# One-core hybrid transformer block: the planner's view of small operations, a group's last squares summed in PSUM, the memory norm one head sooner, a keys unit in a score bank

## The chip, the cores and the metric

The kernel runs as one program on one core of a Trainium2 chip. The metric is the device time of an execution in microseconds; before the change the median of three runs is 766.26 us (766.15 to 769.48).

## The reference

One layer of a streaming encoder on `x` of 512 x 1024 and 256 memory tokens, all float32. Three sub-layers follow each other, each with an RMS norm before it, one after it, and a residual.

1. The token mixer. `h = rms_norm(x)`, one projection `h @ w_in`, whose columns give queries, keys and values for 8 heads of forgetting attention and 8 heads of chunked attention (64 columns a head), and a forget gate. In both kinds
```
s = einsum(q, k) * scale + bias;  s = where(valid, s, NEG_INF)
p = softmax(s);  o = einsum(p, v)
```
over key positions up to the query's own (chunk). The 512 columns of each kind of head are normed by themselves (`rms_norm(o_f, g_fox_out)`, `rms_norm(o_c, g_chunk_out)`), put side by side and multiplied by `w_out`.
2. Cross-attention of 4 heads into the memory: `m = rms_norm(mem, g_mem_kv)`, keys and values from `m @ w_kv`, queries from the normed stream, softmax, output projection `w_o`.
3. A SwiGLU feed-forward: `(silu(g) * u) @ w_down`.

## The kernel before

**Products in three parts.** Float32 products are made of fp32r halves. A number is split into `hi` (a cast) and `lo = number - hi`, and each product is three matmuls, hi·hi, lo·hi and hi·lo (`mm3`, L398 to L402). Weights come in units of 128 x 1024 that are loaded by SyncE's queue (`raw`), cast by ScalarE (`hi`, L381) and subtracted by VectorE (`lo`, L382).

**The attention part.** The 16 heads are worked off in four groups of four: two groups of forgetting heads (n = 0, 1), then two of chunked heads (n = 2, 3), so head 15 is the third head of the last group. `head` (L782 to L828) goes over four query blocks of 128 rows. For each it makes the scores on TensorE (L791, L792) into a PSUM bank of kind `s`; VectorE adds the bias and finds the row's extreme in one instruction (L795, tiles `p` and `nm`); ScalarE takes the exponential (L805); VectorE inverts the row sum (L806, `rc`) and scales (L807); TensorE transposes `p` into a bank of kind `t` (L810); ScalarE casts that to `pth` (L812) and VectorE subtracts for `ptl` (L813). After the four blocks TensorE multiplies `pth` and `ptl` with the values (L819, bank `o`), and ScalarE and VectorE put the result (`ot`, `o`) in place. There are 3 banks of kind `a`, 2 of `s`, 2 of `t` and 1 of `o`.

**After two heads** `pair_out` (L830 to L839) makes `oh` and `ol` for the output projection, and GpSimd (POOL) squares `o`. The first pair's squares go to `sq`; the second pair of a kind, and each later one, squares `o` in place and adds it to `sq` (L839). `group_rs` (L841 to L849) then sums the squares over the partitions with four small matmuls against a column of ones (L844), one for each 128 rows, and makes the reciprocal root of the mean.

**The memory norm.** At n = 3 the memory is loaded (`mm`), squared, and the squares summed (`msq`). `mem_norm` (L851 to L858), traced ahead of the third head of that group, sums over the partitions (L512), makes the reciprocal root, spreads it over the partitions by a matmul (L521), multiplies `mm` in place in eight VectorE instructions (L854), and splits the result in `mT`: hi by ScalarE (L857), lo by VectorE (L858). `mT` is what the keys of the cross-attention are made from: four units of 48 matmuls of 256 columns each (L941 to L962), each unit in a bank `a`, result in `kT`. Ahead of them in the text stands the first half of the output projection (`mix`, L905 to L916, operands `oh`, `ol`, 512 columns), behind them the second half. Four row blocks of `x` are loaded by GpSimd's queue (`xo`).

**What sets the order.** Nothing above is issued in the order of the text. Everything traced ahead of the feed-forward's loop goes through `planned_order` (L90 to L280), a list scheduler. It walks through the program with a model of each engine's time and gives each engine a fixed order: of the instructions that can start at an engine's next free time, the one with the lowest number in the trace order, shifted by `later(n)`, goes first. The model's costs are `duration` (L126), `SIGNAL` and `TO_PE` (L45), the time until TensorE sees another engine's result, and `halves` (L152): when the start partitions of an instruction on VectorE, ScalarE or GpSimd differ from those of the one before, it is charged 28 ns after the former one's end, else it may start a little ahead of that end. `halves` counts operands of more than 8 elements a partition only, so a 128 x 1 operation among wide ones counts as another place. The feed-forward behind the planned part is written out by hand, and is not touched.

Of the kernel before, what the change touches and what calls it, by code (L numbers as in the profile page):

```python
# [8 lines left out]
F32 = mybir.dt.float32  # L9
F32R = mybir.dt.float32r  # L10
AF = mybir.ActivationFunctionType
ALU = mybir.AluOpType
AX = mybir.AxisListType

P = 128
SEQ = 512
# [25 lines left out]
    (ENGINES.DVE, ENGINES.Pool): 80.0, (ENGINES.Activation, ENGINES.Pool): 67.0,  # L42
    (ENGINES.Pool, ENGINES.DVE): 36.0, (ENGINES.Pool, ENGINES.Activation): 34.0,
}
TO_PE, LANDED = 247.0, 60.0  # L45


def number(dims):
    n = 1
    for d in dims:  # L50
        n *= d[1]
    return n
# [37 lines left out]
def planned_order(tc, instructions, homes):  # L90
# [35 lines left out]
    def duration(i):  # L126
        kind = type(i).__name__
        n = number(list(i.outs[0].bass_ap.ap)[1:])
        read = [number(list(a.bass_ap.ap)[1:]) for a in i.ins if tile_of(a)]
        columns = sum(n > 8 and m == 1 for m in read)  # L130
        if i.engine == ENGINES.PE:
            return MATMUL * n if n > 128 else 108.0 if n == 128 else 26.0
        if i.engine == ENGINES.Activation:
            return (284.0 if len(i.outs) > 1 else 160.0) + 0.838 * n + 80.0 * columns
        if i.engine == ENGINES.Pool:
            if n <= 8:
                return 174.0 if kind == "InstTensorCopy" else 1450.0 if n == 1 else 1040.0
            return 25.0 + (0.96 if kind == "InstMemset" else 2.0) * n
        if kind == "InstCustomDveAnt":
            return 245.0 + 0.99 * n  # L140
        if kind == "InstTensorReduce":
            return 158.0 + 1.02 * read[0]
        if kind == "InstMemset":
            return 70.0 + 0.8 * n
        if kind == "InstReciprocal" or n < 8:
            return 158.0
        full = [a for a in i.ins if tile_of(a) and number(list(a.bass_ap.ap)[1:]) > 8]
        if len(full) < 2 and not any(map(in_psum, full)):
            return 213.0 + 0.526 * n
        return 150.0 + 1.046 * n + 60.0 * columns  # L150

    def halves(i):  # L152
        starts = []
        for a in [i.outs[0]] + list(i.ins):
            ap = getattr(a, "bass_ap", None)
            if ap is not None and ap.ap[0][0] and number(list(ap.ap)[1:]) > 8:
                starts.append(ap.offset // ap.ap[0][0])
        return tuple(starts[:2])

    nodes = [i for i in instructions if type(i).__name__ not in ("BassTilePoolBoundary", "InstRegisterMove")]  # L160
    written, read, touched, uses, guests, previous, last_of = {}, {}, {}, {}, {}, {}, {}
# [70 lines left out]
    while any(ready.values()):  # L232
        best = None
        for e, waiting in ready.items():
            starts = [(t, k) for t, k in ((may_start(k), k) for k in waiting) if t is not None]
            if not starts:
                continue
            now = max(free.get(e, 0.0), min(starts)[0])
            if best is None or (now, str(e)) < best[:2]:
                best = now, str(e), e, *min((k, t) for t, k in starts if t <= now + 1.0)  # L240
        _, _, e, k, t = best
        ready[e].remove(k)
        i, start = nodes[k], max(free.get(e, 0.0), t)
        transfer = type(i).__name__ == "InstDMACopy"
        if transfer:
            free[e] = start + ISSUE
            end = landed[e] = max(start + 1900.0, landed.get(e, 0.0)) + 4 * number(i.outs[0].bass_ap.ap) / 300.0
            if e == ENGINES.Pool:
                end += 1500.0
        elif e == ENGINES.PE:  # L250
            cost = duration(i)
            waited = t > free.get(e, 0.0) + 5.0 and cost > 100.0
            free[e] = start + cost + (95.0 if waited else 0.0)
            end = start + max(cost, 60.0) + 170.0
        else:
            if halves(i) != place.get(e, (0, 0)):
                start = max(start, ends.get(e, 0.0) + 28.0)
            place[e] = halves(i)
            end = ends[e] = start + duration(i)
            free[e] = max(start + 20.0, end - TAIL[e])  # L260
        order.setdefault(e, []).append(i)
        for name in used[k]:
            if name not in lasts:
                lasts[name] = {}
                room[homes.tiles[name]].pop(0)
            lasts[name][e, transfer] = end
            uses[name] -= 1
            if not uses[name]:
                room[homes.tiles[name]].append(name)
        for j, in_turn in after[k].items():  # L270
            other = nodes[j].engine
            at[j] = max(at[j], start if in_turn else (start if e == other == ENGINES.PE else end) + reached(e, other, transfer))
            missing[j] -= 1
            if not missing[j]:
                ready.setdefault(other, []).append(j)
# [15 lines left out]
def hybrid_block_kernel(  # L291
# [31 lines left out]
    def bank(tag):  # L323
        serial[0] += 1
        return ps.tile([P, 512], F32, tag=tag, name=f"ps_{tag}{serial[0]}", bufs=BANKS[tag])
# [161 lines left out]
    with tc.tile_pool(name="mix", bufs=1, reuse_waits="tile") as bp:  # L487
# [339 lines left out]
                act.copy(tmp[own, :], acc[other, :])  # L827
                dve.tensor_tensor(out=o[own, :], in0=acc[own, :], in1=tmp[own, :], op=ALU.add)  # L828

        def pair_out(o, gc, oh, ol, sq, first, total):  # L830
            act.activation(oh, o, AF.Copy, scale=gcol(gc))
            dve.scalar_tensor_tensor(
                out=ol, in0=o, scalar=gcol(gc), in1=f32(oh), op0=ALU.mult, op1=ALU.subtract
            )
            if first:
                pool.tensor_tensor(out=sq, in0=o, in1=o, op=ALU.mult)
            else:
                pool.tensor_tensor(out=o, in0=o, in1=o, op=ALU.mult)
                pool.tensor_tensor(out=total, in0=sq, in1=o, op=ALU.add)  # L839

        def group_rs(sq, name):  # L841
            ss = bank("t")
            for t in range(NT):
                pe.matmul(ss[:, t : t + 1], sq[:, t * P : (t + 1) * P], ones, start=True, stop=True)  # L844
            ms = small(NT, "gms")
            dve.tensor_scalar(
                out=ms, in0=ss[:, :NT], scalar1=1.0 / 512.0, scalar2=None, op0=ALU.mult
            )
            return rstd_of(ms, NT, name)  # L849
# [16 lines left out]
        for n, (side, g) in enumerate(order):  # L866
            with later(-20):
                q, kt, kl, v = group_proj(f"{side}{g}")
            if n == 3:
                mT = big.tile([P, 2, KB, NMEM], F32R, tag="sB", name="mT")  # L870
                mm = bp.tile([P, KB, NMEM], F32, tag="V", name="mm", bufs=2)
                nc.gpsimd.dma_start(mm, mem_t.rearrange("(k p) n -> p k n", p=P))
                msq = bp.tile([P, 4, NMEM], F32, tag="T", name="msq", bufs=3)
                for k in range(0, KB, 2):
                    b = msq[:, 2 * (k > 0) : 2 * (k > 0) + 2, :]
                    act.activation(b, mm[:, k : k + 2, :], AF.Square, scale=1.0 / 32.0)
                    if k:
                        pool.tensor_tensor(out=msq[:, 0:2, :], in0=msq[:, 0:2, :], in1=b, op=ALU.add)
            if n == 0:
                gate = forget_gate()  # L880
                oh = ox.tile([P, 8, SEQ], F32R, tag="x1", name="oh")
                ol = ox.tile([P, 8, SEQ], F32R, tag="x2", name="ol")
            if n % 2 == 0:
                sqs.append(bp.tile([P, SEQ], F32, tag="sq", name=f"sq{side}", bufs=1))
            if n == 2:
                with later(300):
                    rs_g.append(group_rs(sqs[0], "rsg0"))
            for b in range(2):
                pr = 2 * g + b
                o = bp.tile([P, SEQ], F32, tag="o", name=f"o{side}{pr}", bufs=2)  # L890
                for h in range(2):
                    hh = 2 * pr + h
                    if n == 3 and 2 * b + h == 2:
                        mem_norm()
                    with later(urge[n] - 295):
                        bias = fox_bias(hh, *gate) if side == 0 else chunk_bias(hh)
                    with later(urge[n]):
                        head(q[b], kt[b], kl[b], v, 2 * b + h, h, bias, o)
                with later(urge[n]):
                    pair_out(  # L900
                        o, (G_FOX, G_CHK)[side] + pr, oh[:, 4 * side + pr, :], ol[:, 4 * side + pr, :],
                        sqs[side], n % 2 == 0 and b == 0, sqs[side],
                    )

        mix = big.tile([P, NT, D], F32, tag="sA", name="mix")  # L905
        with later(-5):
# [12 lines left out]
    with tc.tile_pool(name="cross", bufs=1, reuse_waits="tile") as cp:  # L919
# [21 lines left out]
        with later(-115):  # L941
            for c in range(4):
                hi, lo = unit()
                acc = bank("a")
                for b in range(2):
                    for k in range(KB):
                        cs = slice(b * P, (b + 1) * P)
# [398 lines left out]
        def halves(a):  # L1346
            return a.rearrange("p (t n) -> p t n", t=2)
# [448 lines left out]
```

## Time and profile before

| | |
|---|---|
| median of three runs | 766.26 us |
| the profiled execution | 766.12 us |
| its span, first to last instruction | 764.0 us |
| mean granted TensorE clock | 0.990 |
| TensorE (PE) busy | 747.9 us, 98% |
| VectorE (DVE) busy | 604.2 us, 79% |
| ScalarE (ACT) busy | 444.2 us, 58% |
| GpSimd (POOL) busy | 63.8 us, 8% |
| read from memory | 77.13 MB |

The profile is one execution. A row of a timeline is: start in us, length, engine, line, operation, output<-inputs, size, number of instructions taken together, and in brackets the idle time ahead of it with the instruction that ended it. The number of columns of a matmul is the second of the two sizes. Matmuls are pipelined: one may start before the former has ended, so their pace is read from start to start and not from their lengths. `PEld` is the load of a matmul's stationary operand, beside the matmuls. A row of TensorE's waits is: line, the engine and line waited for, us in total, times, the longest.

### The profile page before, as it was taken

What the parts mean: (1) busy time and instruction counts of PE and PEld (TensorE: products, weight loads), DVE (VectorE), ACT (ScalarE), POOL (GpSimd) and SP (SyncE); (2) the same over time, 40 slices, a digit from 0 to 9 for tenths busy, and PEclk for the clock granted to TensorE, in tenths of its full rate; (3) what the DMA queues carried; (4) which work ended last, traced back from release to release, by engine and by line L of the source; (5) the groups of instructions that cost most, each with busy time, mean ns of one, the idle gap of its engine ahead of it and who ended that gap; (6) DMA issues with size and microseconds to landing.
All of it is one profiled execution on the core that took longest, in us unless ns stands there. A gap on an engine that the chain in (4) does not pass through costs nothing.

```text
span 764.0 us, 12979 instructions
## 1 busy us (share of the span) xinstructions
PE 747.9 (98%) x5024; PEld 682.6 (89%) x5024; DVE 604.2 (79%) x1103; ACT 444.2 (58%) x818; POOL 63.8 (8%) x105
## 2 busy tenths in 40 slices
PE   9999999999989999999999999999999999999996
PEld 9988988888868988888878999999999999999995
DVE  8668899789877578655655598999999999998756
ACT  7558889566955448444564445555555557644321
POOL 1001232100410301000001200000000000000001
PEclk9999999999997999999999999999999999999998
DMA  7522222421412745332341015333333322233222
GB/s 251 149 74 82 55 59 68 110 98 57 138 55 63 250 158 165 112 94 63 121 131 60 28 33 162 111 112 111 112 112 111 111 85 83 83 138 111 84 83 110
DMA packets 60748, 80.05 MB, mean 105 GB/s; under 512 B 2704, under 2 KB 43664, under 8 KB 60688
## 3 DMA queue, kind: packets, MB, share of 16 engines
q1 hardware_dynamic: 59264, 74.49, 31.0%
q0 software_dynamic: 1280, 4.72, 1.7%
q8 instruction: 39, 0.64, 0.4%
q14 instruction: 21, 0.17, 0.1%
q10 hardware_dynamic: 144, 0.02, 0.0%
HBM read 77.13 MB, written 2.10 MB: 104 GB/s over the span
## 4 chain that ended last, share of the span: by engine, by line
PE 88%; issue 4%; ACT 3%; DVE 3%; POOL 1%; DVEq 0%; POOLq 0%; ACTq 0%
PE ps_a L399 14%; PE ps_a L400 14%; PE ps_a L402 14%; PE ps_t L1388 3%; PE ps_t L1385 3%; PE ps_s L1388 3%; PE ps_t L1386 3%; PE ps_s L1386 3%; PE ps_s L1385 3%; PE ps_o L819 3%; PE ps_s L402 2%; PE ps_s L400 2%; PE ps_s L399 2%; PE ps_t L810 2%; PE ps_a L1386 1%
## 5 line engine op out<-in xcount | busy, mean ns | idle before, releaser
L382 DVE TENSOR_TENSOR lo<-raw,hi 128x1024 fp32r<-128x1024 f32 x56 | 69.3, 1242 | 19.3 <-ACT hi L381 19.1
L399 PE MATMUL ps_a<-hTh,hi 128*128 128x512 f32 x192 | 76.5, 399 | 0.2 <-DVE z L618 0.2
L402 PE MATMUL ps_a<-hTh,lo 128*128 128x512 f32 x192 | 76.5, 398 | 0.0
L400 PE MATMUL ps_a<-hTl,hi 128*128 128x512 f32 x192 | 76.3, 397 | 0.0
L381 ACT CAST hi<-raw 128x1024 fp32r<-128x1024 f32 x56 | 57.9, 1049 | 27.2 <-PE ps_a L400 17.5
L1181 DVE TENSOR_TENSOR ring_lo<-sums,ring_hi 128x1024 fp32r<-128x1024 f32 (+1 forms) x39 | 46.7, 1197 | 11.8 <-ACT ring_hi L1180 7.2
L1180 ACT CAST ring_hi<-sums 128x1024 fp32r<-128x1024 f32 (+1 forms) x39 | 40.2, 1030 | 16.5 <-PE ps_s L1386 16.5
L1180 ACT CAST ring_hi<-fraw 128x1024 fp32r<-128x1024 f32 (+1 forms) x26 | 26.5, 1031 | 32.7 <-DVE fraw L1267 24.0
L805 ACT ACTIVATE p<-p,nm 128x128 f32<-128x128 f32 (+1 forms) x64 | 36.3, 568 | 11.3 <-DVE nm L795 10.9
L399 PEld LDWEIGHTS ps_a<-hTh,hi 128*128 128x128 f32 x192 | 36.2, 188 | 6.5 <-ACT V L607 0.4
L402 PEld LDWEIGHTS ps_a<-hTh,lo 128*128 128x128 f32 x192 | 36.2, 188 | 6.3
L400 PEld LDWEIGHTS ps_a<-hTl,hi 128*128 128x128 f32 x192 | 36.2, 188 | 6.1
L1181 DVE TENSOR_TENSOR ring_lo<-fraw,ring_hi 128x1024 fp32r<-128x1024 f32 (+1 forms) x26 | 31.0, 1203 | 11.3 <-ACT ring_hi L1180 11.3
L813 DVE TENSOR_TENSOR ptl<-ps_t,pth 128x128 fp32r<-128x128 f32 (+1 forms) x64 | 30.4, 485 | 7.7 <-ACT pth L812 7.1
L812 ACT CAST pth<-ps_t 128x128 fp32r<-128x128 f32 (+1 forms) x64 | 27.1, 427 | 16.0 <-PE ps_t L810 15.7
L810 PE MATMUL ps_t<-ident,p 128*128 128x128 f32 x160 | 28.9, 280 | 3.5 <-DVE ptl L813 1.6
L810 PEld LDWEIGHTS ps_t<-ident,p 128*128 128x128 f32 x160 | 20.6, 144 | 8.2 <-issue 2.6
L807 DVE TENSOR_SCALAR p<-p,rc 128x128 f32<-128x128 f32 (+1 forms) x64 | 27.3, 427 | 0.1
L1388 PE MATMUL ps_a<-b,ring_lo 128*128 128x256 f32 (+1 forms) x93 | 25.6, 277 | 0.0
L1385 PE MATMUL ps_a<-b,ring_hi 128*128 128x256 f32 x92 | 25.5, 277 | 0.0
L1386 PE MATMUL ps_a<-b,ring_hi 128*128 128x256 f32 x92 | 25.4, 277 | 0.0
L402 PE MATMUL ps_a<-hi,ol 128*128 128x512 f32 x64 | 25.3, 395 | 0.0
(567 smaller groups left out, 2784.2 us busy)
## 6 DMA issues: line engine op xcount, KB each, us to landing
raw<-in_dram SPq DMA_DIRECT2D x64, 512.0 KB, 3.7
fraw<-in_dram SPq DMA_DIRECT2D x26, 512.0 KB, 3.5
place<-in_dram SPq DMA_DIRECT2D x21, 512.0 KB, 4.5
more_room<-in_dram SPq DMA_DIRECT2D x15, 512.0 KB, 4.3
cb<-in_dram SPq DMA_DIRECT2D x8, 256.0 KB, 2.6
xo<-in_dram POOLq DMA_DIRECT2D x4, 512.0 KB, 7.3
out_dram<-yd SPq DMA_DIRECT2D x8, 256.0 KB, 2.0
rawv<-in_dram SPq DMA_DIRECT2D x3, 520.0 KB, 6.0
```

Source lines behind the costliest of these rows:

```text
L381: act.copy(hi[:, j : j + n, :], raw)
L382: dve.tensor_tensor(out=lo[:, j : j + n, :], in0=raw, in1=f32(hi[:, j : j + n, :]), op=ALU.subtract)
L399: pe.matmul(dst, sh, mh, start=first, stop=False)
L400: pe.matmul(dst, sh, ml, start=False, stop=False)
L402: pe.matmul(dst[:, to], sl, mh[:, to], start=False, stop=last)
L805: act.activation(p[:, :n], p[:, :n], AF.Exp, bias=nm, scale=-1.0, accum_out=sm)
L810: pe.transpose(tp[:, k * P : (k + 1) * P], p[:, k * P : (k + 1) * P], ident)
L1180: act.copy(h2, v)
L1181: dve.tensor_tensor(out=l2, in0=v, in1=f32(h2), op=ALU.subtract)
L1385: pe.matmul(dst, w[0][:, k, :], b[:, 0, k, :], start=first and k == 0, stop=False, skip_group_check=more)
L1386: pe.matmul(dst, w[0][:, k, :], b[:, 1, k, :], start=False, stop=False, skip_group_check=more)
L1388: pe.matmul(dst[:, to], w[1][:, k, :], b[:, 0, k, to], start=False, stop=last and k == 3, skip_group_check=more,)
```

## The change

The function lines shift by 3 behind the planner and by up to 10 further down (L791 becomes L794, L844 becomes L849, L854 becomes L862, L858 becomes L866). There are six edits:

- the planner takes 350 instead of 247 ns for TensorE to see a result;
- the planner charges a GpSimd operation on two different tiles 4.1 ns an element instead of 2.0;
- `halves` counts every operand on at least 8 partitions, whatever its length, and an operand that is no tile counts as partition 0; missing operands are filled up;
- the last pair of each kind of head no longer adds its squares to `sq`. `group_rs` takes a list of two tensors, `sq` and the squared `o`, and sums both in PSUM: eight ones matmuls a group instead of four;
- `mem_norm` is traced ahead of the second head of the last group instead of the third;
- the fourth keys unit uses a bank of kind `s` instead of `a`.

```diff
-TO_PE, LANDED = 247.0, 60.0
+TO_PE, LANDED = 350.0, 60.0
...
+            if kind == "InstTensorTensor" and tile_of(i.ins[0]) != tile_of(i.ins[1]):
+                return 25.0 + 4.1 * n
             return 25.0 + (0.96 if kind == "InstMemset" else 2.0) * n
...
-            if ap is not None and ap.ap[0][0] and number(list(ap.ap)[1:]) > 8:
-                starts.append(ap.offset // ap.ap[0][0])
-        return tuple(starts[:2])
+            if ap is not None and ap.ap[0][1] >= 8:
+                whole = number([(0, n) for n in list(ap.tensor.shape)[1:]]) if tile_of(a) else 0
+                starts.append(ap.offset // whole if whole else 0)
+        return (starts + starts + [0, 0])[:2]
...
-            if halves(i) != place.get(e, (0, 0)):
+            if halves(i) != place.get(e, [0, 0]):
...
-        def pair_out(o, gc, oh, ol, sq, first, total):
+        def pair_out(o, gc, oh, ol, sq, first, last):
...
-                pool.tensor_tensor(out=total, in0=sq, in1=o, op=ALU.add)
-
-        def group_rs(sq, name):
+                if not last:
+                    pool.tensor_tensor(out=sq, in0=sq, in1=o, op=ALU.add)
+
+        def group_rs(squares, name):
             ss = bank("t")
             for t in range(NT):
-                pe.matmul(ss[:, t : t + 1], sq[:, t * P : (t + 1) * P], ones, start=True, stop=True)
+                for sq in squares:
+                    pe.matmul(
+                        ss[:, t : t + 1], sq[:, t * P : (t + 1) * P], ones,
+                        start=sq is squares[0], stop=sq is squares[-1],
+                    )
...
-                sqs.append(bp.tile([P, SEQ], F32, tag="sq", name=f"sq{side}", bufs=1))
+                sqs.append([bp.tile([P, SEQ], F32, tag="sq", name=f"sq{side}", bufs=1)])
...
-                    if n == 3 and 2 * b + h == 2:
+                    if n == 3 and 2 * b + h == 1:
                         mem_norm()
...
-                        sqs[side], n % 2 == 0 and b == 0, sqs[side],
+                        sqs[side][0], n % 2 == 0 and b == 0, n % 2 == 1 and b == 1,
                     )
+                if n % 2 == 1 and b == 1:
+                    sqs[side].append(o)
...
-                acc = bank("a")
+                acc = bank("s" if c == 3 else "a")
```

The edits move instructions on every engine between the first heads and the end of the planned part. The rows below are the orders that each engine was given; a row is line, operation, output<-inputs with the tiles' own numbers, size.

VectorE, the memory norm before. `p15` is head 15's second and third query block, `mm` the memory, `L854` its multiplication:
```order
L854 SCALAR_TENSOR_TENSOR mm_2480<-mm_2480,gn_78,ps_t344_2666 128x256
L807 TENSOR_SCALAR p15_1_2700<-p15_1_2700,rc353_2703 128x256
L854 SCALAR_TENSOR_TENSOR mm_2480<-mm_2480,gn_78,ps_t344_2666 128x256
L806 RECIPROCAL rc358_2719<-sm357_2718 128x1
L854 SCALAR_TENSOR_TENSOR mm_2480<-mm_2480,gn_78,ps_t344_2666 128x256
L807 TENSOR_SCALAR p15_2_2716<-p15_2_2716,rc358_2719 128x384
L854 SCALAR_TENSOR_TENSOR mm_2480<-mm_2480,gn_78,ps_t344_2666 128x256
```
VectorE, the same norm after, now among the steps of head 14 (`L862` is the same multiplication):
```order
L862 SCALAR_TENSOR_TENSOR mm_2483<-mm_2483,gn_78,ps_t323_2583 128x256
L816 TENSOR_TENSOR ptl1_411<-ps_t328_2610,pth1_410 128x128
L862 SCALAR_TENSOR_TENSOR mm_2483<-mm_2483,gn_78,ps_t323_2583 128x256
L809 RECIPROCAL rc332_2620<-sm331_2619 128x1
L862 SCALAR_TENSOR_TENSOR mm_2483<-mm_2483,gn_78,ps_t323_2583 128x256
L810 TENSOR_SCALAR p14_1_2617<-p14_1_2617,rc332_2620 128x256
L862 SCALAR_TENSOR_TENSOR mm_2483<-mm_2483,gn_78,ps_t323_2583 128x256
```
The norm has moved by about one head.

TensorE before, ahead of the first keys matmul (`mT` is its operand); `oh` and `ol` are operands of the output projection's first half, and the rest is head 15:
```order
L400 MATMUL ps_a394_2964<-lo11_2847,oh_623 128x512
L402 MATMUL ps_a394_2964<-hi11_2846,ol_624 128x512
L810 MATMUL ps_t354_2708<-ident_69,p15_1_2700 128x128 x2
L810 MATMUL ps_t359_2724<-ident_69,p15_2_2716 128x128 x3
L791 MATMUL ps_s371_2778<-T111_2472,Q111_2396 128x256
L792 MATMUL ps_s371_2778<-L1_417,Q111_2396 128x256
L791 MATMUL ps_s376_2794<-T111_2472,Q111_2396 128x384
L792 MATMUL ps_s376_2794<-L1_417,Q111_2396 128x384
L810 MATMUL ps_t364_2741<-ident_69,p15_3_2733 128x128 x4
L399 MATMUL ps_a402_3014<-mT_2479,hi12_2912 128x256
```
TensorE after, at the same point, the last matmuls of that half of the output projection and the first keys matmul:
```order
L403 MATMUL ps_a394_2966<-lo11_2849,oh_623 128x512
L405 MATMUL ps_a394_2966<-hi11_2848,ol_624 128x512
L794 MATMUL ps_s360_2733<-T111_2475,Q111_2399 128x512
L813 MATMUL ps_t349_2696<-ident_69,p15_0_2688 128x128
L795 MATMUL ps_s360_2733<-L1_417,Q111_2399 128x512
L402 MATMUL ps_a402_3020<-mT_2482,hi12_2914 128x256
```
Before, the first half of the output projection is used up while head 15 has transposes of three blocks and scores left; after, the keys matmuls begin with head 15's first transpose.

TensorE before, the sums of the first kind's squares, four in a row (`hi7` and `hTh` belong to the next projection):
```order
L400 MATMUL ps_a295_2274<-lo7_1789,hTh_82 128x256
L402 MATMUL ps_a295_2274<-hi7_1788,hTl_83 128x256
L399 MATMUL ps_a295_2274<-hi7_1788,hTh_82 128x256
L844 MATMUL ps_t207_1867<-ones_74,sq0_625 128x1 x4
L400 MATMUL ps_a295_2274<-lo7_1789,hTh_82 128x256
```
TensorE after, the second of the eight, on the squares of `o`, and the third:
```order
L402 MATMUL ps_a294_2224<-hi7_1787,hTh_82 128x256
L403 MATMUL ps_a294_2224<-lo7_1788,hTh_82 128x256
L405 MATMUL ps_a294_2224<-hi7_1787,hTl_83 128x256
L849 MATMUL ps_t207_1866<-ones_74,o01_1392 128x1
L849 MATMUL ps_t207_1866<-ones_74,sq0_625 128x1
```
The sum of `o`'s squares stands behind the place where `sq` alone is first summed, with matmuls of the next projection between the first and the second.

## The prediction

> **What bounds the kernel now.** I read the page first, then TensorE's waits, then the stretches around the largest of them, then the instructions in time there.
>
> ```profile
> span 764.0 us, 12979 instructions
> ...
> PE 747.9 (98%) x5024; PEld 682.6 (89%) x5024; DVE 604.2 (79%) x1103; ACT 444.2 (58%) x818; POOL 63.8 (8%) x105
> ...
> PEclk9999999999997999999999999999999999999998
> ```
>
> TensorE is busy 98% of the span, so only what TensorE executes, what it waits for, and its clock can move the end. The granted clock is full in all slices but one in the middle (the thirteenth of 40) and the last. The waits of TensorE say where the missing 2% are:
>
> ```profile
> PE ps_t L810 <- DVE ptl L813: 1.6, 1, 1.6
> PE ps_t L810 <- DVE p L807: 1.5, 1, 1.5
> PE ps_s L791 <- DVE nm L795: 1.5, 1, 1.5
> ...
> PE ps_t L844 <- POOL sq L839: 0.9, 1, 0.9
> ...
> PE ps_o L819 <- DVE ptl L813: 0.4, 1, 0.4
> ...
> PE ps_t L810 <- DVE rc L806: 0.4, 1, 0.4
> ```
>
> The three longest are all for VectorE. They stand together, behind the last matmul of the first output projection:
>
> ```profile
> 224.27 0.39 PE L402 MATMUL ps_a<-hi,ol 128*128 128x512 f32 x1
> ...
> 226.15 0.41 PE L810 MATMUL ps_t<-ident,p 128*128 128x128 f32 x2 [1.49 <-DVE p L807]
> ...
> 228.21 0.90 PE L810 MATMUL ps_t<-ident,p 128*128 128x128 f32 x3 [1.65 <-DVE ptl L813]
> ...
> 231.47 0.69 PE L791 MATMUL ps_s<-T,Q 128*128 128x384 f32 x1 [1.47 <-DVE nm L795]
> ...
> 234.01 0.79 PE L819 MATMUL ps_o<-pth,V 128*128 128x512 f32 x1 [0.25 <-ACT pth L812]
> ```
>
> What VectorE does there is the memory norm (mm, eight times, then mT), between the softmax steps of attention head 15:
>
> ```profile
> 223.00 0.48 DVE L854 SCALAR_TENSOR_TENSOR mm<-mm,gn,ps_t 128x256 f32<-128x256 f32 x1
> ...
> 228.08 0.47 DVE L854 SCALAR_TENSOR_TENSOR mm<-mm,gn,ps_t 128x256 f32<-128x256 f32 x1
> 228.46 0.68 DVE L795 CUSTOM_DVE_ANT_0 p<-ps_s,cb 128x512 f32<-128x512 f32 x1
> ...
> 232.16 2.29 DVE L858 TENSOR_TENSOR mT<-mm,mT 128x2048 fp32r<-128x2048 f32 x1 [0.35 <-ACT mT L857]
> ```
>
> The busy times by stage, with the clock (columns: length, then busy time of PE, PEld, DVE, ACT, POOL, then the clock):
>
> ```profile
> 71.08:140.15 69.07, 68.61 (x412) 60.16 (x411) 62.59 (x172) 58.83 (x141) 16.73 (x33) 1.00 0.26 70
> 224.50:237.54 13.04, 8.10 (x29) 6.33 (x29) 12.48 (x29) 7.40 (x13) 2.32 (x2) 0.61 0.13 41
> 237.54:262.00 24.46, 24.46 (x206) 24.13 (x205) 15.50 (x25) 12.25 (x20) 6.43 (x11) 1.00 0.46 139
> ...
> 207.98:243.14 35.16, 30.22 (x167) 26.03 (x166) 27.61 (x72) 20.75 (x46) 3.03 (x3) 0.85 0.20 61
> ```
>
> In 224.50 to 237.54 VectorE is busy 12.48 of 13.04 us and TensorE does 29 matmuls, at a mean clock of 0.61; in the next row it does 206 in 24.46 us. That stretch is VectorE's, and all the rest is TensorE's.
>
> **The stall, and what takes it away.** Its price needs the pace of matmuls at full clock, from one start to the next:
>
> ```profile
> 217.07 0.40 PE L400 MATMUL ps_a<-lo,oh 128*128 128x512 f32 x1
> 217.30 0.60 PE L810 MATMUL ps_t<-ident,p 128*128 128x128 f32 x4
> 217.74 0.95 PE L512 MATMUL ps_t<-ones,msq 128*128 128x1 f32 x8
> ...
> 220.60 0.33 PE L819 MATMUL ps_o<-pth,V 128*128 128x384 f32 x1
> 220.77 0.34 PE L819 MATMUL ps_o<-ptl,V 128*128 128x384 f32 x1
> 220.95 0.28 PE L819 MATMUL ps_o<-pth,V 128*128 128x256 f32 x1
> 221.06 0.28 PE L819 MATMUL ps_o<-ptl,V 128*128 128x256 f32 x1
> ```
>
> That is 0.23 us for 512 columns, 0.11 for a transpose of 128 (217.30 to 217.74 for four), 0.17 for 384 and 0.11 for 256. The stretch holds 2 matmuls of 512 columns, 4 of 384, 13 of 256 and 9 transposes (the 29th starts at its end): 0.46 + 0.68 + 1.43 + 0.99 = 3.6 us of work in 13.04. The loss is 9.4 us; 4.9 of it are the gaps (1.49 + 1.65 + 1.47 + 0.25), the other 4.5 the lower clock and the pace around them.
>
> Between the matmul that spreads the memory's rstd over the partitions (L521) and the first keys matmul on mT, the order before has 26 matmuls, 3.7 us of work, while VectorE needs 223.00 to 234.45, 11.5 us, from the first mm to the end of mT. The new order has 71 there (52 of 512 columns, 4 of 384, 4 of 256, 11 transposes): 12.0 + 0.7 + 0.4 + 1.2 = 14.3 us. VectorE's rows there are the eight mm at 0.38 (228.08 to 228.46), mT at 2.3, two weight splits, and the softmax steps of head 14:
>
> ```profile
> L382 DVE TENSOR_TENSOR lo<-raw,hi 128x1024 fp32r<-128x1024 f32 x56 | 69.3, 1242 | 19.3 <-ACT hi L381 19.1
> ...
> 230.60 0.55 DVE L813 TENSOR_TENSOR ptl<-ps_t,pth 128x384 fp32r<-128x384 f32 x1
> ```
>
> 3.0 + 2.3 + 2 x 1.2 + about 3.0 for the nine or so steps of head 14 (from 0.1 to 0.68 each) = 10.7 us. Cover of 14.3 for 10.7: some 3 us to spare, so the first keys matmul should find mT ready, and from there on keys matmuls fill head 15 and 16. I take the whole **-9.4**. If the cover failed, the stall would come back there, at the same price.
>
> **The squares.** The Pool addition goes from the path of the first group's rstd:
>
> ```profile
> 149.66 2.13 POOL L839 TENSOR_TENSOR sq<-sq,o 128x512 f32<-128x512 f32 x1
> ...
> 151.84 1.05 PE L844 MATMUL ps_t<-ones,sq 128*128 128x1 f32 x8 [0.85 <-POOL sq L839]
> 152.75 0.36 PE L400 MATMUL ps_a<-lo,hTh 128*128 128x256 f32 x1
> ```
>
> The wait of 0.85 ends with that addition. The new ones matmuls need only the square before it. They also stand earlier: behind the last P.V matmul of head 8 come 13 matmuls of 512 columns and 19 of 256, 5.1 us, where the chain through ot, o, oh, ol and the square took about 5.4 before (144.2 to 149.66). A wait of 0 to 0.4 can stay: I take **-0.7**. In the second group the addition was hidden by keys matmuls, and nothing goes. Each group gets four more ones matmuls; the eight records above (four instructions) take 0.91 us to the next start, so two groups add **+1.8**, at the lower end 0 if they fell into waits, which the order does not show.
>
> A rule on the addition: in this trace one scaling of 384 columns takes 0.96 beside a Pool addition and 0.40 without one.
>
> ```profile
> 203.87 0.96 DVE L807 TENSOR_SCALAR p<-p,rc 128x384 f32<-128x384 f32 x1
> ...
> 213.07 0.40 DVE L807 TENSOR_SCALAR p<-p,rc 128x384 f32<-128x384 f32 x1
> ...
> 203.31 1.30 POOL L878 TENSOR_TENSOR msq<-msq 128x512 f32<-128x512 f32 x1 [0.74 <-ACT msq L876]
> ```
>
> The Trainium skill, "GPSIMD Engine Reference", section "Key points", says that GpSimd shares its SBUF interfaces with VectorE and contends with its two-port and two-input instructions. These rows agree; by it, two Pool additions less would free VectorE for up to 2 x 0.56 us more. I give that nothing, because at the two places TensorE waited for Pool or for nobody, not for VectorE.
>
> **The planner's rules.** The new rules let a small operation (a reciprocal, an rstd) follow a large one without the drain that the old rules charged. So VectorE's list is packed closer, and TensorE's consumers stand earlier. Between the first transpose of head 2 and the last of head 8 (71.08 to 140.15 before) the new order has 42 matmuls fewer: 34 of 512 columns, 6 of 256 or 384 (7.8 + 0.8 = 8.6 us), and two more of 256, moved behind head 8. VectorE's list there is 5 instructions shorter, three splits of 1.2 and two ptl of about 0.5: 4.5 us. So TensorE has 69.07 - 8.6 = 60.5 us of its own pace, and VectorE 62.59 - 4.5 = 58.1 of work: its slack goes from 6.5 us to 2.4. If none of the 6.5 idle was needed, nothing is lost; if all of it was (it waits for ScalarE within each softmax), the stage takes 64.6, +4.1. I take **+1.3**, nearer to zero, because part of the idle time was VectorE waiting for TensorE, which now comes sooner. Likewise heads 14 to 16 (207.98 to 243.14 before): VectorE's 27.61 becomes about 28.9 with the keys' splits, TensorE's 24 us of work becomes about 28.6 with 48 keys matmuls more; nearly level, 0 to +2.5, taken **+0.5**. The small waits of 0.4 (for ptl and rc) are what the longer TO_PE is charged for: 0 to -0.8, **-0.4**. The last cross head's transposes come some 1.8 us sooner after their scores, with a weight cast that waited for its DMA ahead of an exponential on ScalarE:
>
> ```profile
> 380.97 1.05 ACT L381 CAST woh<-raw 128x1024 fp32r<-128x1024 f32 x1 [0.74 <-DMA raw<-in_dram]
> ```
>
> 0 to +1.0, **+0.2**. The score bank for the fourth keys unit frees a bank for the second output projection; no wait in the trace is for that bank, so 0 here, and in the new order it is what lets three keys units sit in the other banks until kT's place is free. Pool's reordered rstd and row loads (a few us ahead of use) cost 0. Behind 262 us the orders are the same but for these.
>
> **The sum.** -9.4 - 0.7 + 1.8 + 1.3 + 0.5 - 0.4 + 0.2 = -6.7. The profiled execution took 766.12 us (span 764.0 and 2.12 around it), the median is 766.26: **759.4 us**. With every unknown at its good end -9.4 - 0.85 + 1.8 - 0.8 = -9.25, 756.9; at its bad end -9.4 - 0.45 + 1.8 + 4.1 + 2.5 + 1.0 = -0.45, 765.7.
>
> **Rivals.** *VectorE becomes the bound of heads 2 to 8 and 14 to 16*, at both upper ends: -9.4 - 0.7 + 1.8 + 4.1 + 2.5 = -1.7, 764.4. For it: 62.59 of 69.07 busy. Against: part of the idle was for TensorE. 0.12.
>
> *The clock stays low there though the gaps go*: only 4.9 of the 9.4 is won, 763.9. Against: the clock is 1.00 in both neighbouring rows and low only here. The Trainium skill, "TensorE: Matmul & The Clock Gate", section "Why this matters for your kernels", puts the fall of the clock at gaps of over about 3 us; the longest gap here is 1.65, so by that rule the gaps are not the cause, and the time is the 763.9. The trace differs: the clock fell among gaps of half that length. 0.03.
>
> *The stall stays* (mT late all the same, the change does nothing to it): 768.8. 0.04.
>
> *Slower: waits for VectorE in heads 2 to 8 come in pairs and halve the clock.* The pair at 224.66 and 226.56 (1.49 and 1.65 within 3.6 us) is followed by the low clock; one such event costs 3.1 + 4.5 = 7.6 us. One brings 767.0, two 774.6: it decides from the second. Against: the slack of 2.4 us is spread over seven heads. 0.05 for two.
>
> **The numbers.** 0.5% is 3.8 us, about what a measurement of this kernel can tell from no change: faster is under 762.4, slower over 770.1. The forecast and its good side have 0.76, the first three rivals together 0.19, all within 0.5%, the slower one 0.05. The range 756.0 to 765.0 takes in the forecast's bounds and the first two rivals.
>
> **What would show it.** Right: clock 1.00 in all middle slices; no wait over 0.6 for L807, L813 or L795; the ones matmuls twice as many, with no wait for Pool; heads 2 to 8 in about 62 us with VectorE over 93% busy. Wrong: a second place under clock 1.00, the first keys matmul waiting for mT, or waits for VectorE that sum to over 4 us in heads 2 to 8.

## The result, and the profile after

The changed kernel takes 757.52 us (756.56 to 757.88, four runs) against 766.89 us for the kernel before (766.15 to 769.48): a ratio of 0.987, 95% interval 0.9844 to 0.9896, so it is faster by 1.3%, and the whole interval lies under 1. The forecast was 759.4, the range 756.0 to 765.0. The profiled execution took 757.27 us with a span of 754.9, 9.1 us less than the span before.

The page of the changed kernel, its first lines:

```profile
span 754.9 us, 13014 instructions
...
PE 744.9 (99%) x5040; PEld 681.8 (90%) x5040; DVE 603.8 (80%) x1103; ACT 445.0 (59%) x818; POOL 59.1 (8%) x103
...
PEclk9999999999999999999999999999999999999998
```

TensorE executes 16 records more and is still busy for 3.0 us less, because the clock is full everywhere but in the last slice. Its waits, longest first:

```profile
PE ps_t L501 <- DVE ones L339: 1.1, 1, 1.1
PE ps_t L813 <- DVE p L810: 0.4, 1, 0.4
PE ps_o L403 <- DVE pt L1084: 0.4, 1, 0.4
PE ps_a L403 <- DVE b L1155: 0.3, 1, 0.3
```

The three waits for VectorE of about 1.5 us are gone, and so is the wait for Pool. The first row is the start of the program. Where the stall was, the end of `mT` on VectorE and the first keys matmul on TensorE:

```profile
217.00 2.29 DVE L866 TENSOR_TENSOR mT<-mm,mT 128x2048 fp32r<-128x2048 f32 x1
```
```profile
222.59 0.28 PE L402 MATMUL ps_a<-mT,hi 128*128 128x256 f32 x1
```

`mT` is ready at 219.29, and its first use comes 3.3 us later: the "some 3 us to spare" of the prediction. The stages (length, then busy time of PE, PEld, DVE, ACT, POOL, then the clock): heads 2 to 8 from first to last transpose; from head 14's first transpose to the first keys matmul; from there, past head 16's last transposes at 239.10, to the fourth keys unit; and the ones matmuls of the second kind.

```profile
73.91:134.15 60.24, 60.04 (x374) 52.98 (x373) 57.60 (x165) 55.93 (x136) 16.07 (x33) 1.00 0.22 63
208.86:222.59 13.73, 13.73 (x70) 11.50 (x68) 12.93 (x35) 9.90 (x21) 0.00 (x0) 1.00 0.23 76
222.59:247.00 24.41, 24.33 (x199) 23.73 (x198) 20.66 (x43) 16.15 (x32) 3.38 (x4) 1.00 0.39 126
...
247.72:249.25 1.53, 1.53 (x17) 1.53 (x15) 1.16 (x1) 1.53 (x4) 0.00 (x0) 1.00 0.51 123
```

TensorE is busy for all but 0.3 of these 100 us. VectorE works 57.60 of 60.24 us in heads 2 to 8, and TensorE waits for it nowhere there (0.44 us before).

### The profile page after: what moved, and what is told of

The parts are those of the page before. It is cut to its first block, busy times and chain, and to the rows that moved or that the text cites. A ratio compares the mean times of both kernels' runs of the same rounds, so it can differ in the third digit from the quotient of the medians.

```text
span 754.9 us, 13014 instructions
## 1 busy us (share of the span) xinstructions
PE 744.9 (99%) x5040; PEld 681.8 (90%) x5040; DVE 603.8 (80%) x1103; ACT 445.0 (59%) x818; POOL 59.1 (8%) x103
## 4 chain that ended last, share of the span: by engine, by line
PE 91%; issue 4%; ACT 2%; DVE 2%; POOL 1%; DVEq 0%; POOLq 0%; ACTq 0%
PE ps_a L403 14%; PE ps_a L402 14%; PE ps_a L405 14%; PE ps_t L1395 3%; PE ps_t L1398 3%; PE ps_s L1396 3%; PE ps_t L1396 3%; PE ps_s L1395 3%; PE ps_s L1398 3%; PE ps_o L822 3%; PE ps_s L403 3%; PE ps_s L405 3%; PE ps_s L402 3%; PE ps_t L813 2%; PE ps_a L1395 1%
## 5 line engine op out<-in xcount | busy, mean ns | idle before, releaser
L815 ACT CAST pth<-ps_t 128x128 fp32r<-128x128 f32 (+1 forms) x64 | 26.8, 423 | 10.6 <-PE ps_t L813 10.0
L810 DVE TENSOR_SCALAR p<-p,rc 128x128 f32<-128x128 f32 (+1 forms) x64 | 30.1, 470 | 0.2
L403 PE MATMUL ps_a<-lo,oh 128*128 128x512 f32 x64 | 25.3, 395 | 0.0
L402 PE MATMUL ps_a<-hi,oh 128*128 128x512 f32 x64 | 25.2, 394 | 0.0
```

The costliest lines, as they stand in the source:

```text
L402: pe.matmul(dst, sh, mh, start=first, stop=False)
L403: pe.matmul(dst, sh, ml, start=False, stop=False)
```

## The experiments

The question was which of the six edits brings the 9 us, and what the others do. The theory of the prediction was cover: enough matmuls between the spread of the memory's rstd and the first keys matmul. Each kernel ran beside the kernel before; ratios are to that, with the 95% interval. The kernel before took 766.23 to 766.48 us beside the experiments and 766.89 beside the changed kernel, so two times measured beside different runs of it do not tell two kernels apart when they differ by less than 1 us.

**The norm a head sooner, alone.**
```diff
-                    if n == 3 and 2 * b + h == 2:
+                    if n == 3 and 2 * b + h == 1:
```


> The kernel before with the one edit that traces the memory norm a head sooner; planner rules, squares and banks stay as before. Theory (cover): in this order 51 matmuls, about 10.5 us, stand between the spread of the memory's rstd and the first keys matmul, and VectorE's list from the first mm to the end of mT is 7.4 us by row durations (the same sum for the kernel after gives 9.4 and took 10.8, so about 8.8 here). The cover is longer, so the stall goes with this edit alone: no wait over 0.6 us for VectorE around 210 to 240 us, clock 1.00, 757.5 to 759.5 us (the wait for Pool of 0.9 stays, the four extra ones matmuls a group are not there). Rival (the planner's new rules carry the gain): the stall stays, 764 to 767 us, clock under 1.00 in the middle.

Measured: 772.04 us, ratio 1.0069 (1.0056 to 1.0082). Both theories were wrong: it is slower. The wait for `mT` is gone, as the cover said, but TensorE stalls later, behind head 16. Its timeline there (start, length):

```profile
246.16 0.60 PE L810 MATMUL ps_t<-ident,p 128*128 128x128 f32 x4
248.81 0.50 PE L819 MATMUL ps_o<-pth,V 128*128 128x512 f32 x1 [2.05 <-ACT pth L812]
250.37 0.50 PE L819 MATMUL ps_o<-ptl,V 128*128 128x512 f32 x1 [1.07 <-DVE ptl L813]
...
257.15 1.86 PE L844 MATMUL ps_t<-ones,sq 128*128 128x1 f32 x8 [5.45 <-POOL sq L839]
260.06 0.58 PE L399 MATMUL ps_a<-mT,hi 128*128 128x256 f32 x1 [1.05 <-DVE kT L954]
```

The keys matmuls are the filler for heads 15 and 16. Started a head sooner, three units (144 matmuls) are used up before head 16's last P.V; the fourth waits for a bank `a`, which only kT's copies free. Before, 85 keys matmuls of the second and third unit stood behind that P.V, 52 of them ahead of the ones matmuls. Now nothing does, so the chain o, square, addition and ones is bare: 2.05 + 1.07 + 5.45 + 1.05 us of waits, and the clock is at 0.50 for 13.6 us:

```profile
251.70:265.30 13.60, 7.10 (x32) 7.02 (x33) 3.56 (x7) 2.75 (x5) 6.64 (x12) 0.50 0.43 144
```

**The planner's three edits, alone.**
```diff
-TO_PE, LANDED = 247.0, 60.0
+TO_PE, LANDED = 350.0, 60.0
...
+                return 25.0 + 4.1 * n
...
-            if ap is not None and ap.ap[0][0] and number(list(ap.ap)[1:]) > 8:
+            if ap is not None and ap.ap[0][1] >= 8:
```


> The kernel before with the planner's three edits alone (350 ns to TensorE, the Pool cost, the new rule for start partitions); the norm is traced where it was. Theory (cover): 45 matmuls, about 9.1 us, stand ahead of the first keys matmul, against a VectorE list of 7.7 us by row durations, about 9.0 in time: the cover is just level, so a wait of 0 to 1 us may stay, clock 1.00, 758 to 761 us. Rival (it is the norm's place in the trace that counts): the stall and the low clock stay, 764 to 767 us.

Measured: 757.48 us, ratio 0.9881 (0.9866 to 0.9895): the whole gain of the change without its other three edits, and better than expected. The longest wait:

```profile
PE ps_a L403 <- DVE mT L861: 1.4, 1, 1.4
```

The cover was a little short and not level: some 9.2 us of matmuls against the 10.6 that VectorE took, and the wait is about the difference. The clock is full. The wait for Pool of 0.85 us behind head 8 is gone too, although Pool still adds the squares.

**The start-partition rule alone, and the time to TensorE alone.** First the rule (`halves`):
```diff
-            if ap is not None and ap.ap[0][0] and number(list(ap.ap)[1:]) > 8:
-                starts.append(ap.offset // ap.ap[0][0])
+            if ap is not None and ap.ap[0][1] >= 8:
+                whole = number([(0, n) for n in list(ap.tensor.shape)[1:]]) if tile_of(a) else 0
+                starts.append(ap.offset // whole if whole else 0)
```


> The kernel before with the new rule for start partitions alone (247 ns to TensorE, old Pool cost, norm where it was). Theory: of the planner's edits this one makes the cover: 44 matmuls, 8.9 us, stand ahead of the first keys matmul, as with all three planner edits (45, which gave 757.5 with a wait of 1.4 for mT). So clock 1.00, a wait for mT of 1 to 2 us, 757.3 to 759.5 us. Rival (the longer time to TensorE is needed too): the stall stays, 763 to 767 us.

Measured: 758.36 us, ratio 0.989 (0.9873 to 0.9906), with these longest waits:

```profile
PE ps_a L401 <- DVE mT L859: 1.8, 1, 1.8
PE ps_t L845 <- POOL sq L840: 1.5, 2, 0.9
```

The two waits for Pool are 0.66 us behind head 8 and 0.87 behind head 16.

Then the number:
```diff
-TO_PE, LANDED = 247.0, 60.0
+TO_PE, LANDED = 350.0, 60.0
```


> The kernel before with the one edit from 247 to 350 ns in the planner's time to TensorE. Theory (cover): 24 matmuls, 4.3 us, stand ahead of the first keys matmul, fewer than before, against a VectorE list of 9.9 us by row durations (8.9 before): the stall and the low clock stay, 765 to 769 us. Rival (any move of the order frees it, or the longer time carries part of the gain): under 763 us.

Measured: 765.26 us, ratio 0.9986 (0.9977 to 0.9995). The stall stays, in another shape:

```profile
PE ps_t L810 <- DVE p L807: 3.4, 1, 3.4
PE ps_a L400 <- DVE mT L858: 1.5, 1, 1.5
```

So of the planner's edits the rule for start partitions makes the gain: it moves the cover from 26 matmuls to 44, and the number alone moves it to 24. The cover count told both cases rightly ahead of the runs, and its size holds too: 8.9 us of matmuls against the 10.8 that VectorE took leave 1.9, and the wait for `mT` is 1.8. What the number does is another thing: with it, no wait for Pool is left at either place, here and with all three planner edits. The edit of Pool's cost was not run alone.

**The change with the norm late.**
```diff
-                    if n == 3 and 2 * b + h == 1:
+                    if n == 3 and 2 * b + h == 2:
```


> The changed kernel with the memory norm traced where it was before. Theory (cover): the same 45 matmuls, 9.1 us, against about 9.0 as with the planner's edits alone, so most of the gain stays: 757.5 to 760.5 us, and the first keys matmul waits under 1.5 us. Rival (the norm's place carries the gain): 764 to 767 us with the clock under 1.00 in the middle.

Measured: 758.90 us, ratio 0.9899 (0.9886 to 0.9913). It waits 1.4 us for `mT` (L866) as with the planner's edits alone; that is what the sooner norm is worth in the changed kernel.

**The change with the old planner.** The three planner edits undone.
```diff
-TO_PE, LANDED = 350.0, 60.0
+TO_PE, LANDED = 247.0, 60.0
...
-            if ap is not None and ap.ap[0][1] >= 8:
+            if ap is not None and ap.ap[0][0] and number(list(ap.ap)[1:]) > 8:
```


> The changed kernel with the planner's three edits undone: norm a head sooner, squares in PSUM, fourth keys unit in a score bank, under the old rules. Theory: with the norm sooner alone, the keys matmuls were used up by the end of head 16 and TensorE waited 5.5 us for the squares and 3.6 for the last scores' steps; here the fourth keys unit in a score bank and the ones matmuls without the addition put 46 keys matmuls, 5.2 us, behind head 16's last P.V, against about 3.5 us that the chain to the squares takes. So no wait over 1 us there, clock 1.00, 757.5 to 760 us. Rival (the old rules pack heads 15 and 16 too loosely whatever covers them): 764 us or more.

Measured: 761.58 us, ratio 0.9932 (0.992 to 0.9944), over the expected range and under the rival's. The wait behind head 16 is only 0.5 us, as expected, but there is one of 1.5 for `mT`, and the clock is at 0.50 for 3.4 us behind the ones matmuls, which the theory had not in it. The cover tells the first: 46 matmuls, 9.3 us, against 10.2 on VectorE, whose first `mm` started 1.3 us behind the spread and not 0.65 as in the changed kernel. So the other three edits take 4.9 us off under the old rules: the start-partition rule is enough for the gain, but not the only way to a large part of it.

**The norm and the planner, without squares and bank.**
```diff
-                    if n == 3 and 2 * b + h == 2:
+                    if n == 3 and 2 * b + h == 1:
...
+            if ap is not None and ap.ap[0][1] >= 8:
```


> The kernel before with the planner's rules and the norm a head sooner, but without the squares in PSUM and without the score bank. Theory: behind head 16's last P.V stand 36 keys matmuls, 4.1 us, and then the ones matmuls, which wait for the addition on Pool (5.6 us behind that P.V with the norm alone): a wait of about 1.5 us for Pool, then about 1 us for kT, and the clock falls for one step of 3.4 us (1.7 us): 757.5 - 1.8 + 0.8 + 2.5 + 1.7 = 760.7, 759.5 to 762 us. Rival (with the planner's rules the squares and the bank are not needed): 756.0 to 757.5 us.

Measured: 762.13 us, ratio 0.9943 (0.9928 to 0.9958), just over the expected range. Behind head 16:

```profile
246.64 0.28 PE L405 MATMUL ps_a<-mT,lo 128*128 128x256 f32 x1
248.55 1.36 PE L847 MATMUL ps_t<-ones,sq 128*128 128x1 f32 x8 [1.64 <-POOL sq L842]
251.75 0.58 PE L402 MATMUL ps_a<-mT,hi 128*128 128x256 f32 x1 [1.85 <-DVE kT L957]
```
```profile
249.20:256.00 6.80, 4.95 (x24) 4.87 (x24) 3.63 (x7) 1.08 (x3) 3.77 (x9) 0.50 0.88 301
```

The wait for Pool is the expected one, that for kT 1.85 and not 1 us, and the clock fell for two steps of 3.4 us and not one. So with the norm sooner, the squares in PSUM and the score bank are needed: together they are worth some 5 us here (762.13 against 757.52).

**The fourth keys unit back in a bank `a`.**
```diff
-                acc = bank("s" if c == 3 else "a")
+                acc = bank("a")
```


> The changed kernel with the fourth keys unit in a bank of kind a again. Theory: with three units in the three banks, the fourth must wait for kT's copies: behind head 16 there are 36 keys matmuls, 4.1 us, then the ones matmuls; the first copy of kT is done some 1.5 us behind them, so TensorE waits 1 to 2 us there: 758.5 to 760 us. Rival (the prediction's 0 for this edit): 757.2 to 757.9 us.

Measured: 760.11 us, ratio 0.9913 (0.99 to 0.9927); the span is 757.8 us, 2.9 more than with the score bank. The wait is the expected one, and the clock adds to it:

```profile
248.25 0.36 PE L849 MATMUL ps_t<-ones,o 128*128 128x1 f32 x2
249.94 0.39 PE L402 MATMUL ps_a<-mT,hi 128*128 128x256 f32 x1 [1.33 <-DVE kT L964]
```
```profile
246.89:249.94 3.05, 1.72 (x14) 1.64 (x14) 2.04 (x5) 3.05 (x5) 0.90 (x4) 1.00 0.58 182
250.20:253.60 3.40, 3.40 (x18) 3.40 (x18) 2.09 (x3) 0.05 (x1) 3.20 (x7) 0.50 0.72 227
253.60:257.00 3.40, 3.40 (x31) 3.40 (x31) 0.00 (x0) 0.00 (x0) 0.08 (x1) 1.00 1.03 381
```

18 matmuls stand in 3.4 us at clock 0.50 and 31 in the next 3.4 us. The wait costs 1.3 us and the clock some 1.4 (13 matmuls of 0.11 us), together the 2.6 us that the time lies over the changed kernel. The expectation had the wait alone, and the time is just over its range.

**The squares in PSUM for the first kind only.**
```diff
-                        sqs[side][0], n % 2 == 0 and b == 0, n % 2 == 1 and b == 1,
+                        sqs[side][0], n % 2 == 0 and b == 0, n == 1 and b == 1,
                     )
-                if n % 2 == 1 and b == 1:
+                if n == 1 and b == 1:
```


> The changed kernel with the squares summed in PSUM for the first kind of head only; for the second kind the last addition goes back to Pool. Theory: the four extra ones matmuls of the second kind (8 records, 0.9 us) are work of TensorE with nothing in return, because its addition lay beside keys matmuls: 0.9 us faster than the changed kernel, 756.2 to 757.0 us. Rival: the addition comes late now or slows VectorE beside it, and TensorE waits for it: 757.5 to 758.5 us.

Measured: 755.65 us, ratio 0.9857 (0.9843 to 0.9871); the span is 754.1, 0.8 us under that of the changed kernel. It is a little under the expected range, and no wait for Pool comes in. TensorE has 8 records less and is busy 0.7 us less (744.2 against 744.9). So the four extra ones matmuls of the second kind are a loss of 0.7 to 0.9 us. The medians lie 1.9 us apart, but the intervals of the two ratios overlap. This kernel has the shortest time of all that were run.

**`mT`'s lo half subtracted twice on VectorE** (the same values; the planner is charged half for each, so that the order stays nearly as it was).
```diff
-            dve.tensor_tensor(out=mT[:, 1], in0=mm, in1=f32(mT[:, 0]), op=ALU.subtract)
+            for _ in range(2):
+                dve.tensor_tensor(out=mT[:, 1], in0=mm, in1=f32(mT[:, 0]), op=ALU.subtract)
...
+        if i.engine == ENGINES.DVE and n == 2048:
+            return 2292.0 / 2
```


> The changed kernel with mT's lo half subtracted twice on VectorE (2.3 us more work, same values; the planner is charged half of it for each, so that the order stays nearly the same). Theory: mT has 3.3 us to spare, so the keys matmuls do not wait for it; but head 14's last scaling, 0.7 us ahead of its transposes, comes 2.3 us later, so TensorE waits 1.5 to 2 us there, once, and the clock stays 1.00: 759 to 760 us. Rival (a wait of that length is enough for the clock to fall): a slice under clock 1.00 and 762 us or more.

Measured: 758.38 us, ratio 0.9893 (0.9878 to 0.9907). A little under the expected range, with one wait of the expected size at another step (the scores' `nm` of head 15 and not head 14's transposes):

```profile
222.40 0.41 PE L796 MATMUL ps_s<-T,Q 128*128 128x384 f32 x1 [1.46 <-DVE nm L800]
```

The clock stays at 1.00. So the keys had the room that the cover gave them, and VectorE's softmax steps behind `mT` had less; and one wait of 1.46 us between wide matmuls does not lower the clock.

**Every ones matmul twice** (each sum counted double, its scale halved).
```diff
-                for sq in squares:
+                for n, sq in enumerate(squares + squares):
...
-                out=ms, in0=ss[:, :NT], scalar1=1.0 / 512.0, scalar2=None, op0=ALU.mult
+                out=ms, in0=ss[:, :NT], scalar1=1.0 / 1024.0, scalar2=None, op0=ALU.mult
```


> The changed kernel with every ones matmul of the group sums issued twice (each sum counted double, the scale halved, the same values): 16 instructions more, 32 records. Theory on the price: each record is 0.11 us of TensorE with nothing beside it, so 3.6 us more, 761.1 us, if the clock stays. Theory on the clock: a stretch of one-column matmuls counts as idle; 15 of them in a row, 3.3 us and no wait at all, make the clock fall for one or two steps of 3.4 us behind each group, 1.7 to 3.4 us more each: 763 to 768 us with slices under 1.00 near 150 or 250 us. Rival (only waits lower the clock): clock 1.00, 760.5 to 761.7 us. Second rival (the ones matmuls cost nothing, they fall into slack): 757.5 us.

Measured: 765.45 us, ratio 0.9984 (0.9969 to 0.9998), with runs from 760.51 to 767.02. No wait over 0.3 us is added, and yet:

```profile
252.67:255.20 2.53, 2.53 (x26) 2.53 (x24) 1.23 (x1) 2.53 (x5) 0.00 (x0) 1.00 0.54 206
255.35:262.10 6.75, 6.75 (x33) 6.75 (x33) 3.17 (x6) 0.06 (x1) 3.79 (x9) 0.50 0.63 205
```

TensorE is busy all the time in both rows, and the clock falls to 0.50 while the ones matmuls still run, 2.6 us behind the first of the row, for 6.8 us; at 146 us it does so 2.3 us behind the first. So a wait is not needed: one-column matmuls in a row act on the clock as idle time does. The one execution of 760.51 us had a mean clock of 0.998, the other eleven 0.988 to 0.994; so the 32 records alone cost some 3 us (3.6 were expected), and the rest goes with the clock.

**300 ns to TensorE, on the fastest kernel.**
```diff
-TO_PE, LANDED = 350.0, 60.0
+TO_PE, LANDED = 300.0, 60.0
```


> The kernel with the squares in PSUM for the first kind only (755.65 us), with 300 ns to TensorE instead of 350. Theory: cover and VectorE list ahead of the keys matmuls stay (14.2 us for a list of 8.8), so only small waits of 0.4 to 0.6 us late in the cross-attention can move: 755 to 756.5 us. Rival (the longer time is what keeps the transposes from waiting in heads 2 to 16): 757 us or more.

Measured: 756.47 us, ratio 0.9871 (0.9855 to 0.9888), at the upper end of the theory's range and overlapping the kernel with 350. Inconclusive: it does not pay, and its loss is not clear of the measurement.

## Why the prediction was right, and where not

**What bounds the kernel** was right: TensorE's waits and its clock, with VectorE in the one stretch of the memory norm.

**The stall, -9.4**, was right in full. The gaps, 4.9 us of it, are gone; the rest shows in TensorE's busy time, which is 3.0 us less though 16 records more take 1.8. From head 14's first transpose to head 16's last:

```profile
208.86:239.10 30.24, 30.16 (x201) 27.41 (x200) 28.53 (x71) 21.82 (x47) 2.39 (x2) 1.00 0.32 105
```

The predicted cover of 14.3 us against 10.7 on VectorE, with some 3 to spare, was 14.3 against 10.8 in the trace, with 3.3. What the prediction did not do is to say which edit brings the cover. It costed the planner's rules only as a loss and counted all of the change's order as one. The runs split it: the start-partition rule alone takes 8 us off (766.48 to 758.36), the sooner norm alone adds 6 (766.34 to 772.04), although it clears the stall at `mT`. The prediction gave the stall's end to the order of all six edits, which it had counted rightly; that one planner rule is enough for it, it did not foresee.

**Heads 2 to 8, +1.3, heads 14 to 16, +0.5, and the late cross head, +0.2**, are the terms that were too large. The stage of heads 2 to 8 takes 60.24 us, where TensorE's own pace was given as 60.5, with VectorE at 57.60 of work (58.1 predicted): 0 and not +1.3. Of the 6.5 us that VectorE idled there before, 2.6 are left, and TensorE waits for none of them. The profile puts most of the idle time before down to ScalarE; that TensorE stood behind it, as the prediction argued, is not shown. In heads 14 to 16 VectorE has 28.53 us of work (28.9 predicted), but TensorE 30.16 and not 28.6, so the two are not level and nothing is lost. In the last cross head the expected wait came, 0.41 us for `pt` (L1084), but one of 0.58 for `y` behind it (L1125 before) went, why is open, and one for `b` (L1145 before) is 0.1 shorter: -0.3 in all. Together these terms came out 2.3 us lower than forecast.

**The squares, -0.7 and +1.8**, held as sizes: no wait for Pool (-0.85), 16 records more. The cause given for the first is not shown. The wait behind head 8 is gone with the 350 ns alone, with the planner's edits alone, and with these and the norm, and in all three Pool still adds the squares. So the first kind's ones matmuls in PSUM may gain nothing either; the changed kernel without them was not run. That the second kind gains nothing held, by the 0.7 to 0.9 us that its four ones matmuls cost. But "the addition was hidden by keys matmuls" is true only while keys matmuls stand there; with the norm sooner and no score bank it was a wait of 1.64 or 5.45 us.

**The small waits, -0.4**, held: both (0.44 for ptl, 0.35 for rc) are gone, and one of 0.42 came at head 13's second block. With these sizes the sum is -9.4 - 0.85 + 1.8 - 0.4 - 0.3 = -9.15, against 9.1 between the spans.

**The score bank, 0**, was the step that failed as a statement on an edit: the prediction took the price from the trace of before, where the keys began late and no wait for that bank stands. It named what the bank is for in the new order, and gave that no price. In the order of the change it is worth 2.9 us of span.

**The rivals.** VectorE as the bound did not come. The low clock went with the gaps, against the rival's 763.9. The slower rival named the right mechanism (waits in pairs that halve the clock) and the wrong place: it happened with the norm alone, behind head 16, where the filler had run out. The range, said to take in the forecast's bounds, ended at 765.0, below the bad end of 765.7; the result did not need it.

## What to carry to other kernels

When a step is moved sooner so that a filler can start sooner, count what is left of the filler at the end of the stage: the keys matmuls that closed the gap at `mT` were missing 25 us later, and the move alone was slower. Cost a change of a planner's rules by the orders that it makes, edit by edit; here one rule on tiny operations was enough, and the three edits outside the planner cancel as nearly as the runs can tell (757.48 without them, 757.52 with them): in the order of the change the norm sooner gains 1.4 us but needs the score bank, and the extra ones matmuls cost some of it again. An idle share of an engine beside the one that bounds the stage is no price by itself.

## What the runs showed of the hardware

The low clock comes in steps. It lasted 3.4 us (the fourth unit in bank `a`), 6.8 (norm and planner, and the ones matmuls twice) and 13.6 (norm alone), and just over 10 in the kernel before: multiples of 3.4 us, each costing up to half of that, 1.4 us in the first case. The Trainium skill, "TensorE: Matmul & The Clock Gate", section "What's actually happening", gives a free-running window of 3413 ns; the runs agree. Since it runs by itself, the same kernel can lose one step more or less: that fits the spread of 760.51 to 767.02 us of the kernel with the ones matmuls twice, though the phase was not measured.

What lowers the clock is not the length of a gap alone. One gap of 1.46 us between wide matmuls, or one of 1.8, left it at 1.00; a gap of 1.33 us behind 1.5 us of one-column matmuls lowered it, one of 0.48 ahead of as many did (the old planner), and so did 2.3 to 2.6 us of one-column matmuls with no gap, while 1.5 us of them with no gap did not (the changed kernel). In the kernel before it fell within the second of two gaps of 1.5 and 1.65 us, with two transposes between them. The Trainium skill, "TensorE: Matmul & The Clock Gate", section "Why this matters for your kernels", speaks of gaps of over about 3 us. The runs differ, unless such matmuls, and the two transposes, are counted as gap; no run here settles that. Each of these cases is one profile, and where the steps of 3.4 us lay in it was not chosen.

VectorE's scalings beside a Pool addition were slower still than in the rows of before. In the changed kernel:

```profile
198.61 1.46 DVE L810 TENSOR_SCALAR p<-p,rc 128x256 f32<-128x256 f32 x1
...
212.43 0.34 DVE L810 TENSOR_SCALAR p<-p,rc 128x256 f32<-128x256 f32 x1
```
```profile
198.63 1.29 POOL L886 TENSOR_TENSOR msq<-msq 128x512 f32<-128x512 f32 x1 [0.78 <-ACT msq L884]
```

The same scaling takes 1.46 beside the addition of the memory's squares and 0.34 alone, and the next transpose, of head 13, waits 0.4 us for it: the one wait for VectorE that is left in the attention part.
